# Recurrent branch of a hybrid encoder block: score blocks by 2 and by 8 in one step, a group's outputs and transposes in one step each

## The chip, the core and the metric

The kernel runs on one core of a Trainium2 chip. The metric is the device time of one execution in microseconds (us); the time of a kernel is the median of its runs. The engines of the core are TensorE (PE in the profile, with PEld for the loading of weights into it), VectorE (DVE), ScalarE (ACT), GpSimd (POOL) and SyncE (SP), which issues most of the loads.

## What is computed

One block over 256 tokens of width 2048: an HGRN2 recurrence and a chunked attention side by side, gated and merged, then a squared-ReLU MLP. All inputs are float32. The change lies in the recurrence, whose eight heads have keys and values of width 128:

```python
f = jax.nn.sigmoid(hf)
g = lb + (1.0 - lb) * f
log_g = jnp.log(g)
kk = 1.0 - g
q = jax.nn.silu(hq) * (HG_DK ** -0.5)
...
b = jnp.cumsum(gc, axis=2)
o_inter = jnp.einsum('bhtk,bhkv->bhtv', qc * jnp.exp(b), S)
diff = b[:, :, :, None, :] - b[:, :, None, :, :]
decay = jnp.exp(jnp.where(causal[:, :, None], diff, -jnp.inf))
scores = jnp.einsum('bhtk,bhtsk,bhsk->bhts', qc, decay, kc)
o_intra = jnp.einsum('bhts,bhsv->bhtv', scores, vc)
...
o = rms_norm(o, hg_norm_w) * jax.nn.silu(hg)
```

`hq`, `hf`, `hi` (the values) and `hg` (the output gate) are column blocks of the normed input times `w_in`.

## The kernel before

A float32 product is made of products of rounded parts. `weights` loads pieces of a weight from SP's queue into `raw`, ScalarE rounds each to `wh` (L91), VectorE subtracts to get `wl` (L92), and these two run ahead of TensorE through six `raw` and four `wh` and `wl` buffers at high priority. `gemm` (`hi`, `hg`) issues three matmuls for each k-tile and half of the tokens (L136 to L138), six to a k-tile; `gemm_t` (`hf`, `hq`, `aq`, `ak`) puts the channels on the partitions and issues two high products (L178) and two low ones (L183) to a k-tile.

The recurrence is worked out for pairs of heads, four of them (0 to 3); pairs 0 and 1 are group 0, pairs 2 and 3 group 1. Instead of carrying a state from chunk to chunk the kernel makes whole score matrices of 128 by 128 tokens, and one of the second half of the tokens against the first. They are put together from blocks:

- `diagonal` (L367) makes single tokens and their neighbours from `q` and `kk`.
- `factors(i, B)` (L376) makes, for blocks by B = 2, 8 and 32 tokens, the decayed keys `kl` and queries `qr` on VectorE with exponentials on ScalarE. The last instruction of `qr` is L404.
- `level(i, B)` (L407) multiplies them: for each of two heads a tile `ps` of one PSUM bank, two float32 matmuls into it (L415, each of which the profile shows as two instructions), and three predicated copies by VectorE into the score matrix `sd` (L422).
- `factors128` (L424) and `level128` (L443) do the same for the second half against the first, with matmuls at L447 and a copy to `so` by ScalarE (L449).
- `hgrn_out` (L466) has `outputs` (scores times values into `po`, L478 and L479; a square on ScalarE, L483; a sum, a small scaling and a power on VectorE, VectorE and POOL, L484, L98 and L99; four products with the factor and the gate `gw` on VectorE, L490) and `finish` (four transposes into `tpo`, L498, split into the two parts of the activation `ya`).

PSUM has eight banks: two accumulators of two banks for the weight products, two banks `ps_tp` for transposes and the last scores, two banks `ps_sm` for scores and outputs.

None of these steps runs as a stage of its own. They are put into a queue, `behind`, by `later`, each with a gap, and the products take them out: `tick` is called ahead of every k-tile with 2 by `gemm` and with 1 by `gemm_t`, and issues the first step of the queue when its gap is used up; what a tick overshoots is not carried over. So the small matmuls of a step stand in TensorE's program between two k-tiles of a weight product. `scores` (L523) queues the seven steps of a pair, `group` (L541) the outputs of a group, and hands back the transposes to be queued later.

The instructions are given to the engines in this order by a scheduler, which may put an instruction of higher priority, or one that is ready, ahead of another on the same engine. Semaphores are set by it too. `po` and `ps` are tiles of pools with two buffers, `osq` has one.

Of the kernel before, what the change touches and what calls it, by code (L numbers as in the profile page):

```python
# [8 lines left out]
F32 = mybir.dt.float32  # L9
# [7 lines left out]
P = 128  # L17
T = 256
NM = T // P
# [17 lines left out]
def bc(ap, pos, n):  # L37

    dims = [list(d) for d in ap.ap]
    dims.insert(pos, [0, n])  # L40
    return bass.AP(tensor=ap.tensor, offset=ap.offset, ap=dims)
# [9 lines left out]
def tile_hybrid_block(  # L51
# [14 lines left out]
    ps_acc, ps_tp, ps_sm = [cm.__enter__() for cm in ps_cms]  # L66
# [85 lines left out]
    def later(*steps):  # L152
        behind.extend([n, f] for n, f in steps)
# [10 lines left out]
    def gemm_t(rhs, w, n0, nkt, what):  # L164

        acc = new_acc(what)
        for a in weights(w, n0, nkt, T, what):
            tick(1)
            mm_t(acc, rhs, nkt, *a)
        return acc  # L170
# [168 lines left out]
    def v_chunk(g):  # L339
        acc = gemm(xT, w_in_n, C_HI + g * NC, KD, f"hi{g}")  # L340
        vs = []
        for m in range(NM):
            v = hp.tile([P, NC], F32, name=f"v{g}{m}", tag="tok", bufs=7)
            nc.scalar.activation(v, acc[:, m, :], AF.Copy, scale=rstd[:, m:m + 1])
            vs.append(v)
        return vs

    def hg_chunk(g):
        acc = gemm(xT, w_in_n, C_HG + g * NC, KD, f"hg{g}")
        gws = []  # L350
        for m in range(NM):
            s = hp.tile([P, NC], F32, name=f"gw{g}{m}", tag="tok", bufs=7)
            nc.scalar.activation(s, acc[:, m, :], AF.Sigmoid, scale=rstd[:, m:m + 1])
            nc.vector.scalar_tensor_tensor(s, acc[:, m, :], rstd[:, m:m + 1], s, op0=ALU.mult, op1=ALU.mult)
            s3 = s.rearrange("p (h d) -> p h d", d=DK)
            nc.vector.tensor_tensor(s3, s3, bc(hgw, 1, NH), op=ALU.mult)
            gws.append(s)
        return gws

    def hgrn_scores(n, made):  # L360

        kk, b, q = made["kk"], made["b"], made["q"]
        sd = hp.tile([P, 2, NM, P], F32, name=f"sd{n}", tag="sd", bufs=2)
        so = hp.tile([P, 2, P], F32, name=f"so{n}", tag="so", bufs=2)
# [42 lines left out]
        def level(i, B):  # L407
            kl, qr, _, _ = held[i]
            klf = kl.rearrange("p n v b -> p (n v b)")
            qrf = qr.rearrange("p n k b -> p (n k b)")  # L410
            for h in range(2):
                ps = ps_sm.tile([P, NM, 192], F32, name=f"ps{n}_{B}{h}", tag="sm")
                for m in range(NM):
                    a = 2 * h + m
                    nc.tensor.matmul(ps[:, m, :], klf[:, a * P:(a + 1) * P], qrf[:, a * 192:(a + 1) * 192],  # L415
                                     start=True, stop=True)
                dst = sd[:, h].rearrange("p m (n w) -> p m n w", w=4 * B)
                src = ps.rearrange("p m (n w) -> p m n w", w=6 * B)
                mask = masks[:, i, :].rearrange("p (n w) -> p n w", w=6 * B).bitcast(I32)
                for d0, k0, k1 in ((1, 0, 3), (2, 3, 5), (3, 5, 6)):  # L420
                    k = slice(k0 * B, k1 * B)
                    nc.vector.copy_predicated(dst[:, :, :, d0 * B:], bc(mask[:, :, k], 1, NM), src[:, :, :, k])  # L422
# [20 lines left out]
        def level128():  # L443
            kc, ql = held["128"]
            ps = ps_tp.tile([P, 2, P], F32, name=f"ps{n}_128", tag="tp")
            for h in range(2):
                nc.tensor.matmul(ps[:, h, :], kc[:, h].rearrange("p v b -> p (v b)"),  # L447
                                 ql[:, h].rearrange("p v b -> p (v b)"), start=True, stop=True)
            nc.scalar.copy(so, ps)  # L449

        f = [lambda i=i, B=B: factors(i, B) for i, B in enumerate(LEVELS)]
        l = [lambda i=i, B=B: level(i, B) for i, B in enumerate(LEVELS)]

        def first():
            diagonal()
            f[0]()

        def final():
            l[2]()
            level128()  # L460

        return (sd, so), [first, f[1], l[0], f[2], l[1], factors128, final]

    ya = []

# [38 lines left out]
    def fq(u):  # L504
        if u == 0:
            f, z = f0, z0
        elif u == 1:
            f, z = f1, z1
        else:
            f, z = h2(f"f{u}"), h2(f"zq{u}")  # L510
            add_parts(f, gemm_t(xT, w_in_t, C_HF + u * T, KD, f"hf{u}"))
            add_parts(z, gemm_t(xT, w_in_t, C_HQ + u * T, KD, f"hq{u}"))
        made = {}

        def decay():
            made["g"], made["kk"], made["b"] = hf_pair(u, f)

        def query():
            made["q"] = hq_pair(u, z, made["g"])

        return made, decay, query

    def scores(n, made, gap, first=None, between=()):  # L523

        sc = []
        steps = []

        def one(i):
            if not i:
                out, fs = hgrn_scores(n, made)  # L530
                sc.extend(out)
                steps.extend(fs)
            steps[i]()

        todo = [(gap if i or first is None else first, lambda i=i: one(i)) for i in range(7)]
        for at, f in between:
            todo.insert(at, (gap, f))
        later(*todo)
        return sc

    def group(g, s0, s1, vs, gws, gap, gap2):  # L541
        parts = {}

        def outputs(h0, sc):
            parts[h0] = hgrn_out(g, h0, sc, vs, gws)
            parts[h0][0]()

        later(*[(gap, lambda h0=h0, sc=sc: outputs(h0, sc)) for h0, sc in ((0, s0), (2, s1))])
        return [(gap2, lambda h0=h0: parts[h0][1]()) for h0 in (0, 2)]

    ya += [new_act(f"ya{g}") for g in range(2)]
    a0, a1 = fq(0), fq(1)
    a0[1]()
    a0[2]()
    s0 = scores(0, a0[0], 5, 15, ((5, a1[1]), (8, a1[2])))
    vs0 = v_chunk(0)
    s1 = scores(1, a1[0], 4)
    gws0 = hg_chunk(0)
    turns0 = group(0, s0, s1, vs0, gws0, 6, 6)
    a2 = fq(2)  # L560
    later((3, a2[1]), (3, a2[2]), *turns0)
    s2 = scores(2, a2[0], 4)
    a3 = fq(3)
    later((3, a3[1]), (3, a3[2]))
    vs1 = v_chunk(1)
    s3 = scores(3, a3[0], 4)
    gws1 = hg_chunk(1)
    later(*group(1, s2, s3, vs1, gws1, 3, 6))
    acc_q = [gemm_t(xT, w_in_t, C_AQ + i * T, KD, f"aq0{i}") for i in range(2)]
    while behind:  # L570
        tick(9)
# [639 lines left out]
```

## Time and profile before

| | |
|---|---|
| time, median of 3 runs | 1389.49 us (1389.38 to 1389.76) |
| profiled execution: time | 1389.94 us |
| profiled execution: span of the core | 1388.1 us |
| granted TensorE clock, mean | 0.999 |
| first and last score matmul (L371, L415) | 62.3 and 206.1 us |
| score blocks, L415: instructions, median duration | 96, 326 ns |
| transposes of the outputs, L498: instructions, mean duration | 16, 272 ns |
| products hi0 and hg0 | from 53 to 102 us |
| products hf2, hq2, hf3, hq3 | from 102 to 157 us |
| products hi1 and hg1, then aq | from 157 to 211 us, from 211 us |

The times in the profile are microseconds from the start of the span, durations of one instruction nanoseconds where a view says "mean". Matmuls are pipelined: the recorded durations of neighbours overlap, so what one costs is read from the distance between starts. In a timeline a row gives the start, the duration of the whole row, the engine, the line of the kernel, the operation, the tiles as out<-in, the shapes, and in brackets the idle time before it with what ended it.

### The profile page before, as it was taken

The numbers are of one execution on the slowest core, as the hardware profiler recorded it, in microseconds if no ns is written. First come the engines' busy times: TensorE is split into PE (matmuls) and PEld (weight loads), VectorE is DVE, ScalarE is ACT, GpSimd is POOL, SyncE is SP. The second block draws the span as 40 slices with busy tenths as digits, with TensorE's granted clock in tenths as the row PEclk, the third lists the DMA queues.
The fourth block names the chain that finished last, engine by engine and source line by source line (L and its number), as shares of the span: only waits on it lengthen the run. The fifth ranks groups of instructions, "written<-read, shape, count | busy, mean of one in ns | idle before, by whom it ended". The sixth has DMA issues, their size and how long they took to land.

```text
span 1388.1 us, 18593 instructions
## 1 busy us (share of the span) xinstructions
PE 1376.7 (99%) x6550; PEld 1143.5 (82%) x6550; DVE 1137.7 (82%) x1417; ACT 922.7 (66%) x1185; POOL 143.4 (10%) x227
## 2 busy tenths in 40 slices
PE   9999999999999999999999999999999999999997
PEld 8889888878778888888888888888888888888886
DVE  7897988876878775698998977879877888878886
ACT  6765645665676664346777766678666876668864
POOL 3000001101100000001211011200011001110200
PEclk9999999999999999999999999999999999999999
DMA  9654446685669886558979789988899889998892
GB/s 328 235 178 141 163 166 239 169 284 169 175 199 284 261 266 226 189 168 273 301 215 310 245 259 300 261 255 244 251 298 295 248 223 263 276 297 265 255 276 105
DMA packets 124077, 331.61 MB, mean 239 GB/s; under 512 B 11072, under 2 KB 11840, under 8 KB 123600
## 3 DMA queue, kind: packets, MB, share of 16 engines
q1 hardware_dynamic: 103696, 265.59, 54.4%
q0 software_dynamic: 19568, 64.04, 23.5%
q8 instruction: 51, 0.84, 0.2%
q10 hardware_dynamic: 720, 0.81, 0.2%
q14 instruction: 42, 0.34, 0.1%
HBM read 271.67 MB, written 10.49 MB: 203 GB/s over the span
## 4 chain that ended last, share of the span: by engine, by line
PE 89%; DMA 5%; DVE 3%; issue 2%; ACT 1%; POOL 0%; POOLq 0%; SPq 0%; ACTq 0%; DVEq 0%
PE acc_ak L178 2%; PE acc_aq L178 2%; PE acc_hf L178 2%; PE acc_hq L178 2%; PE ps L415 1%; PE acc_ak L183 1%; PE acc_hg L137 1%; PE acc_hi L137 1%; PE acc_bb L136 1%; PE acc_hi L138 1%; PE acc_hg L136 1%; PE acc_bb L137 1%; PE acc_ba L136 1%; PE acc_hi L136 1%; PE acc_ba L138 1%
## 5 line engine op out<-in xcount | busy, mean ns | idle before, releaser
L178 PE MATMUL acc_aq<-act_x,wh_aq 128*128 128x512 f32 x128 | 41.7, 402 | 0.0
L178 PE MATMUL acc_hf<-act_x,wh_hf 128*128 128x512 f32 x128 | 40.8, 400 | 0.1
L178 PE MATMUL acc_hq<-act_x,wh_hq 128*128 128x512 f32 x128 | 40.7, 400 | 0.0
L178 PE MATMUL acc_ak<-act_x,wh_ak 128*128 128x512 f32 x128 | 40.4, 397 | 0.0
L91 ACT CAST wh_bb<-raw_bb 128x1024 fp32r<-128x1024 f32 x16 | 16.9, 1054 | 23.3 <-PE acc_ba L138 17.7
L92 DVE TENSOR_TENSOR wl_bb<-raw_bb,wh_bb 128x1024 fp32r<-128x1024 f32 x16 | 19.6, 1223 | 14.8 <-ACT wh_bb L91 14.8
L91 ACT CAST wh_ba<-raw_ba 128x1024 fp32r<-128x1024 f32 x16 | 16.8, 1052 | 19.9 <-PE acc_bb L138 13.8
L92 DVE TENSOR_TENSOR wl_aq<-raw_aq,wh_aq 128x1024 fp32r<-128x1024 f32 x16 | 19.5, 1222 | 12.5 <-ACT wh_aq L91 12.5
L92 DVE TENSOR_TENSOR wl_ba<-raw_ba,wh_ba 128x1024 fp32r<-128x1024 f32 x16 | 19.5, 1223 | 11.6 <-ACT wh_ba L91 11.6
L183 PEld LDWEIGHTS acc_hq<-act_x,wl_hq 128*128 128x128 f32 x128 | 23.4, 188 | 6.6 <-DVE wl_hq L92 1.4
L91 ACT CAST wh_aq<-raw_aq 128x1024 fp32r<-128x1024 f32 x16 | 16.7, 1051 | 17.1 <-PE acc_hg L138 7.3
L183 PEld LDWEIGHTS acc_hf<-act_x,wl_hf 128*128 128x128 f32 x128 | 23.4, 188 | 5.5 <-DVE wl_hf L92 0.3
L183 PEld LDWEIGHTS acc_ak<-act_x,wl_ak 128*128 128x128 f32 x128 | 23.5, 188 | 5.3
L183 PEld LDWEIGHTS acc_aq<-act_x,wl_aq 128*128 128x128 f32 x128 | 23.3, 188 | 5.1 <-issue 0.3
L92 DVE TENSOR_TENSOR act_u<-tp_u,act_u 128x512 fp32r<-128x512 f32 x32 | 21.9, 685 | 4.7 <-ACT act_u L91 4.2
L183 PE MATMUL acc_hq<-act_x,wl_hq 128*128 128x256 f32 x128 | 24.7, 280 | 1.0 <-DVE wl_hq L92 1.0
L136 PE MATMUL acc_hg<-wh_hg,act_x 128*128 128x512 f32 x64 | 25.6, 400 | 0.0
L183 PE MATMUL acc_aq<-act_x,wl_aq 128*128 128x256 f32 x128 | 25.6, 284 | 0.0
L136 PE MATMUL acc_hi<-wh_hi,act_x 128*128 128x512 f32 x64 | 25.5, 399 | 0.0
L92 DVE TENSOR_TENSOR wl_hf<-raw_hf,wh_hf 128x1024 fp32r<-128x1024 f32 (+2 forms) x21 | 20.5, 976 | 6.1 <-ACT wh_hf L91 5.7
L91 ACT CAST wh_ak<-raw_ak 128x1024 fp32r<-128x1024 f32 x16 | 16.8, 1051 | 12.9 <-PE acc_aq L178 5.5
L136 PE MATMUL acc_bb<-wh_bb,act_yb 128*128 128x512 f32 x64 | 25.2, 393 | 0.0
(1928 smaller groups left out, 5237.3 us busy)
## 6 DMA issues: line engine op xcount, KB each, us to landing
raw_hi<-in_w_in_n_dram SPq DMA_DIRECT2D x16, 512.0 KB, 4.5
raw_hg<-in_w_in_n_dram SPq DMA_DIRECT2D x16, 512.0 KB, 3.5
raw_aq<-in_w_in_t_dram SPq DMA_DIRECT2D x16, 512.0 KB, 3.7
raw_ak<-in_w_in_t_dram SPq DMA_DIRECT2D x16, 512.0 KB, 4.8
raw_ba<-in_w_branch_a_dram SPq DMA_DIRECT2D x16, 512.0 KB, 4.6
raw_bb<-in_w_branch_b_dram SPq DMA_DIRECT2D x16, 512.0 KB, 4.7
raw_hf<-in_w_in_t_dram SPq DMA_DIRECT2D x12, 512.0 KB, 3.6
raw_hq<-in_w_in_t_dram SPq DMA_DIRECT2D x12, 512.0 KB, 4.0
```

The lines of the kernel that those rows point to most:

```text
L91: casts[:] = [(copy or nc.scalar.copy)(hi, src)]
L92: return nc.vector.tensor_tensor(lo, src, hi.bitcast(F32), op=ALU.subtract)
L136: nc.tensor.matmul(acc, hi, wh, start=first, stop=False, skip_group_check=True)
L137: nc.tensor.matmul(acc, hi, wl, start=False, stop=False, skip_group_check=True)
L138: nc.tensor.matmul(acc, lo, wh, start=False, stop=last, skip_group_check=True)
L178: nc.tensor.matmul(acc[:, cb, :], wh[:, cb * P:(cb + 1) * P], r.rearrange("p u t -> p (u t)"), start=kt == 0, stop=last)
L183: nc.tensor.matmul(acc[:, cb, 0:T], wl[:, cb * P:(cb + 1) * P], r[:, 0, :], start=False, stop=False)
L415: nc.tensor.matmul(ps[:, m, :], klf[:, a * P:(a + 1) * P], qrf[:, a * 192:(a + 1) * 192], start=True, stop=True)
```

## The change

The steps of a pair become six: the multiplications of the blocks by 2 and by 8 are issued in one step, `near`, after both their factors; those by 32 and `level128` stay one step, now called `far`. The two `ps` tiles of the blocks by 8 come from `ps_tp` instead of `ps_sm`. The outputs of a group's two pairs are one step, `both`, and their transposes one step, `finish`. The gaps are changed with it: from 5 and 4 to 6 for scores, from 6 to 8 for the transposes; the gaps of the outputs, 6 and 3, stay, but there is one of them to a group instead of two. The places at which pair 1's decay and query are put into the queue of pair 0 move from 5 and 8 to 4 and 7.

```diff
@@ level
-                ps = ps_sm.tile([P, NM, 192], F32, name=f"ps{n}_{B}{h}", tag="sm")
+                home, tag = (ps_tp, "tp") if i == 1 else (ps_sm, "sm")
+                ps = home.tile([P, NM, 192], F32, name=f"ps{n}_{B}{h}", tag=tag)
@@ hgrn_scores
-        def final():
+        def near():
+            l[0]()
+            l[1]()
+
+        def far():
             l[2]()
             level128()
-        return (sd, so), [first, f[1], l[0], f[2], l[1], factors128, final]
+        return (sd, so), [first, f[1], near, f[2], factors128, far]
@@ scores
-        todo = [(gap if i or first is None else first, lambda i=i: one(i)) for i in range(7)]
+        todo = [(gap if i or first is None else first, lambda i=i: one(i)) for i in range(6)]
@@ group
-        later(*[(gap, lambda h0=h0, sc=sc: outputs(h0, sc)) for h0, sc in ((0, s0), (2, s1))])
-        return [(gap2, lambda h0=h0: parts[h0][1]()) for h0 in (0, 2)]
+        def both():
+            outputs(0, s0)
+            outputs(2, s1)
+
+        def finish():
+            for h0 in (0, 2):
+                parts[h0][1]()
+
+        later((gap, both))
+        return [(gap2, finish)]
@@ tile_hybrid_block
-    s0 = scores(0, a0[0], 5, 15, ((5, a1[1]), (8, a1[2])))
+    s0 = scores(0, a0[0], 6, 15, ((4, a1[1]), (7, a1[2])))
-    s1 = scores(1, a1[0], 4)
+    s1 = scores(1, a1[0], 6)
-    turns0 = group(0, s0, s1, vs0, gws0, 6, 6)
+    turns0 = group(0, s0, s1, vs0, gws0, 6, 8)
-    s2 = scores(2, a2[0], 4)
+    s2 = scores(2, a2[0], 6)
-    s3 = scores(3, a3[0], 4)
+    s3 = scores(3, a3[0], 6)
-    later(*group(1, s2, s3, vs1, gws1, 3, 6))
+    later(*group(1, s2, s3, vs1, gws1, 3, 8))
```

## The prediction

> **What bounds the kernel now.** I read the page's engine shares and its chain first, then who TensorE (PE) waited for, then the stretch of the recurrent branch in windows, then its instructions one by one.
>
> ```profile
> PE 1376.7 (99%) x6550; PEld 1143.5 (82%) x6550; DVE 1137.7 (82%) x1417; ACT 922.7 (66%) x1185; POOL 143.4 (10%) x227
> ```
>
> ```profile
> PE 89%; DMA 5%; DVE 3%; issue 2%; ACT 1%; POOL 0%; POOLq 0%; SPq 0%; ACTq 0%; DVEq 0%
> ```
>
> ```profile
> PE ps_warm L81 <- DVE warm L79: 1.1, 1, 1.1
> PE acc_hq L183 <- DVE wl_hq L92: 1.0, 1, 1.0
> PE tpp L618 <- DVE sb L614: 0.3, 2, 0.2
> PE acc_ga0c L136 <- ACT acc_ga0c L759: 0.3, 1, 0.3
> ```
>
> The columns of the last are the sum, the times and the longest wait in us. TensorE is the bound, and none of its waits lies in the recurrent branch (62 to 226 us). What the change can win there is only TensorE time that is neither a matmul at full rate nor a wait: the seams between the stream of weight products and the small float32 matmuls put in between. What it can lose is a wait that does not exist today. VectorE (DVE) is the candidate for that:
>
> ```profile
> 157.00:183.00 26.00, 26.00 (x125) 22.24 (x124) 25.96 (x66) 17.68 (x24) 0.00 (x0) 1.00 0.45 147
> ```
>
> Behind the stretch and its length stand PE, weight loads, VectorE, ScalarE, POOL, the granted clock and DMA: VectorE is busy 25.96 of 26.00 us, the clock is 1.00. TensorE does not notice, since VectorE runs ahead of it.
>
> **The seam of a score step.** This is the first pair's blocks by 2 (L415, eight instructions: two for each float32 matmul), start and duration:
>
> ```profile
> 71.55 0.39 PE L138 MATMUL acc_hi<-wh_hi,act_x 128*128 128x512 f32 x1
> 71.78 1.46 PE L415 MATMUL ps<-qr,kl 128*128 128x192 f32 x8
> 72.94 0.53 PE L136 MATMUL acc_hi<-wh_hi,act_x 128*128 128x512 f32 x1
> 73.31 0.40 PE L137 MATMUL acc_hi<-wl_hi,act_x 128*128 128x512 f32 x1
> 73.54 0.39 PE L138 MATMUL acc_hi<-wh_hi,act_x 128*128 128x512 f32 x1
> ```
>
> Starts count, since durations overlap. Undisturbed, a product matmul starts 0.23 us after the last (71.55 to 71.78, 73.31 to 73.54). The eight take 72.94 - 71.78 = 1.16 us, 0.145 each; the first product matmul behind them takes 73.31 - 72.94 = 0.37 instead of 0.23. The seam is 0.14 us, at the return only. Two blocks in one step keep all sixteen small instructions and pay it once: 0.14 x 4 pairs = **0.56 us** saved.
>
> **The seams of outputs and transposes.**
>
> ```profile
> 130.64 0.61 PE L479 MATMUL po<-v,sd 128*128 128x128 f32 x4
> ...
> 131.90 0.70 PE L178 MATMUL acc_hf<-act_x,wh_hf 128*128 128x512 f32 x2
> 132.44 0.40 PE L183 MATMUL acc_hf<-act_x,wl_hf 128*128 128x256 f32 x2
> 132.68 0.62 PE L178 MATMUL acc_hf<-act_x,wh_hf 128*128 128x512 f32 x2
> 133.14 0.40 PE L183 MATMUL acc_hf<-act_x,wl_hf 128*128 128x256 f32 x2
> ...
> 145.88 0.60 PE L498 MATMUL tpo<-ident,o 128*128 128x128 f32 x4
> 146.24 0.71 PE L178 MATMUL acc_hq<-act_x,wh_hq 128*128 128x512 f32 x2
> 146.79 0.40 PE L183 MATMUL acc_hq<-act_x,wl_hq 128*128 128x256 f32 x2
> ```
>
> Two high products take 133.14 - 132.68 = 0.46; behind an output step 132.44 - 131.90 = 0.54, behind a pair's transposes 146.79 - 146.24 = 0.55. Each seam is 0.08, and each of the two groups loses one of either kind: 0.08 x 4 = **0.32 us**. The step itself is 131.90 - 130.64 = 1.26, the transposes 146.24 - 145.88 = 0.36; both are unchanged. All seams together: **0.88 us**, the whole gain there is to have. No matmul, eviction, exponential or DMA is removed.
>
> **What moves, and what it could wait for.** The gaps count ticks: one for a k-tile of a transposed product (133.14 - 132.44 = 0.70 us), two for a k-tile of the others. Counted through the queue of steps with its rounding, the places become:
>
> Blocks by 2 of the first pair stay ahead of k-tile 13 of hi0, and the blocks by 8, six k-tiles later before, now stand right behind them. Their factors are VectorE work:
>
> ```profile
> 70.40 1.22 DVE L92 TENSOR_TENSOR wl_hg<-raw_hg,wh_hg 128x1024 fp32r<-128x1024 f32 x1 [0.23 <-ACT wh_hg L91]
> 71.54 0.55 DVE L402 TENSOR_TENSOR qr<-q,er 128x384 f32<-128x384 f32 x1
> 72.01 0.68 DVE L382 TENSOR_TENSOR el<-b 128x512 f32<-128x512 f32 x1
> 72.61 0.42 DVE L403 TENSOR_TENSOR qr<-qr,rr 128x256 f32<-128x256 f32 x1
> 72.94 1.22 DVE L92 TENSOR_TENSOR wl_hg<-raw_hg,wh_hg 128x1024 fp32r<-128x1024 f32 x1
> 74.08 0.28 DVE L404 TENSOR_TENSOR qr<-qr,rr 128x128 f32<-128x128 f32 x1
> ```
>
> The last piece of the blocks by 8 (L404) is done at 74.36, and TensorE would want it at 72.94: a wait of **1.42 us**, behind which the rest of hi0 queues. Against the full price: L382 of the next factors (blocks by 32) stands between L402 and L403 of this one, so the order on an engine is arranged by what is ready, not by the code alone; if TensorE's order is arranged so too, product matmuls go ahead of the blocks by 8, and only the 0.14 of this one seam is lost. Bounds 0.14 to 1.42; I take 0.2, as that row shows the arranging. In the other three pairs a whole gap of six ticks (4.2 us) lies between the factors and the joint step, and VectorE works on them long before; second and fourth pair I put at nothing, the third, inside the full stretch quoted above, between 0 and 0.7 (one k-tile), and take 0. The twelve predicated copies behind a joint step queue on VectorE ahead of weight splits (wl); what covers these is their lead, as the first wl_hg above ends at 71.62 and TensorE starts on it at
>
> ```profile
> 77.17 0.39 PE L136 MATMUL acc_hg<-wh_hg,act_x 128*128 128x512 f32 x1
> ```
>
> which is 5.5 us later. Without that cover a split (1.22) would come on the path. Accumulators: the blocks by 8 take the transposes' buffers, so four are in use at once and none is waited for; two outputs fill the two score buffers, whose next user comes over 10 ticks later; so nothing.
>
> The outputs of the first group are transposed 14 ticks after them (9.8 us, the second pair 0.4 later), and the chain behind outputs is long: before, the second pair was left by TensorE at the first row and ready at the end of the second,
>
> ```profile
> 137.42 0.70 PE L178 MATMUL acc_hf<-act_x,wh_hf 128*128 128x512 f32 x2
> ```
>
> ```profile
> 147.70 0.34 DVE L490 SCALAR_TENSOR_TENSOR o<-po,ro,gw 128x128 f32<-128x128 f32 x1
> ```
>
> 148.04 - 137.42 = 10.6 us against 10.2: 0 to 0.4 of wait. The second group has less room. Before:
>
> ```profile
> 216.83 0.70 PE L178 MATMUL acc_aq<-act_x,wh_aq 128*128 128x512 f32 x2
> ...
> 225.73 0.60 PE L498 MATMUL tpo<-ident,o 128*128 128x128 f32 x4
> ```
>
> ```profile
> 217.11 0.60 ACT L483 ACTIVATE osq<-po 128x512 f32<-128x512 f32 x1 [0.65 <-PE po L479]
> ```
>
> ```profile
> 221.77 0.16 DVE L98 TENSOR_SCALAR os<-os 128x4 f32<-128x4 f32 x1
> 223.06 0.87 DVE L490 SCALAR_TENSOR_TENSOR o<-po,ro,gw 128x128 f32<-128x128 f32 x3 [1.12 <-POOL ro L99]
> ...
> 225.57 0.34 DVE L490 SCALAR_TENSOR_TENSOR o<-po,ro,gw 128x128 f32<-128x128 f32 x1
> ```
>
> Chain 225.91 - 216.83 = 9.1 us, room 225.73 - 216.83 = 8.9: just in time. Now the room is 8 ticks and the first pair's transposes, 8 x 0.70 + 0.36 = 6.0. At the old length TensorE waits **3.1 us**, with the rest of the aq products behind it. It need not be so long: ScalarE had its square at 217.11, yet the next small step came at 221.77. The second pair's chain lay behind the first pair's on VectorE and behind the gate of hg1, which TensorE finishes two and five k-tiles ahead of the two outputs before, but six and the last scores ahead of them after. From 221.77 on the chain needs 4.1. Bounds 0 to 3.1; I take 0.3, since the shorter end is what the work needs. The outputs of the fourth pair also follow its last scores more closely, 3 ticks and the third pair's outputs behind, 2.1 + 1.26 = 3.4 us. Six copies have to be through by then:
>
> ```profile
> 206.00 1.58 DVE L422 COPY_PREDICATED sd<-masks,ps 128x192 f32<-128x192 int32 x6
> ```
>
> With a split ahead of them, 1.58 + 1.22 = 2.8: nothing. POOL's power instructions move with the outputs, and its bias loads for the attention are issued behind the last of them, now earlier; SP's queue is not passed.
>
> **Sum.** -0.88 + 0.2 + 0.3 = -0.4 us. The profiled execution has a span of 1388.1 and a time of 1389.94, 1.84 outside the span; the median of the runs is 0.45 below it. Applied to the median: 1389.49 - 0.4 = **1389.1**.
>
> **Rivals.**
> 1. *One wait at full price.* Only the first pair's: -0.88 + 1.42 = +0.5, 1390.0. Only the second group's: -0.88 + 3.1 = +2.2, 1391.7. For it: VectorE's order above, and a chain that was just in time. Against: the arranging, and the gate's work that leaves the chain.
> 2. *Slower: the transposes of the second group wait for their outputs, the chain being as long as in the first group.* 10.6 - 6.0 = 4.6 of wait, -0.88 + 4.6 = +3.7, 1393.2. It decides over 0.2% (2.8 us) from a chain of 6.0 + 0.9 + 2.8 = 9.7 us. For it: one square buffer and two outputs at once, so that ScalarE and VectorE hold each other up in order. Against: the second group has no factors of a next pair beside it.
>    The Trainium skill (TensorE: Matmul & The Clock Gate, Part 1: The HAM clock gate) says that TensorE's clock falls to half after an idle window of about 3.4 us. By that rule such a wait would cost another 1.7 us (an estimate: one window at half rate), 1395; no run here shows it yet.
> 3. *The steps are taken apart again* by the arranging, or the seam stays between two blocks: no gain, no wait, 1389.5. For it: L382 above. Against: every step of TensorE that I followed stands at its counted k-tile.
> 4. *Faster by over 0.2%.* Beyond 0.88 there would have to go 1.9 us of waits, and after the start-up TensorE's are 0.3 + 0.3. Only a changed order in the later stages could do it, 1386.5.
>
> **How the numbers follow.** About 0.2%, 2.8 us, is what a measurement of this kernel can tell from no change. Forecast 0.46 (its own range 1388.4 to 1390.0); rival 1: 0.19; rival 2: 0.20; rival 3: 0.10; rival 4: 0.05. Rivals 1 and 3 lie within the bound, so the same: 0.46 + 0.19 + 0.10 = 0.75; slower 0.20, faster 0.05. The range, 1387.8 to 1393.0, leaves out rival 4 and most of rival 2, and holds the bounds of both waits taken singly.
>
> **What would show it.** Right: in each pair sixteen L415 instructions in a row, about 2.33 us, and one matmul of 0.37 behind them; 24 output instructions and then eight transposes in a row; no new line among TensorE's waits; the hpool stage ending 0.4 to 0.9 us earlier. Wrong: a gap ahead of the blocks by 8 near 73 us, or ahead of L498 in the aq products with L490 as its releaser, or a wl split that comes late in the stretch where VectorE is full.

## The result, and the profile after

The changed kernel takes **1390.76 us** (median of 22 runs, 1390.44 to 1394.22), the kernel before 1389.32 on the same chip (22 runs, 1388.4 to 1390.94): a ratio of 1.0012, with a 95% interval of 1.0007 to 1.0018. That is +1.44 us (by the interval 1.0 to 2.5), inside the bound of 0.2% and inside the range, but the sign is not the forecast one: a loss that can be told from nothing, where a gain of 0.4 was expected.

The page of the changed kernel, busy time by engine and the chain that ended last:

```profile
PE 1376.5 (99%) x6550; PEld 1143.3 (82%) x6550; DVE 1138.3 (82%) x1417; ACT 922.6 (66%) x1184; POOL 143.2 (10%) x227
...
PE 93%; DMA 2%; DVE 2%; ACT 1%; issue 1%; POOL 0%; POOLq 0%; SPq 0%; ACTq 0%; DVEq 0%
```

The engine totals show nothing: the same counts as before, but for one record of ScalarE (1184 against 1185). The difference stands in the list of whom TensorE waited for (sum in us, times, longest), of the changed kernel:

```profile
PE acc_hq L183 <- DVE wl_hq L92: 1.1, 1, 1.1
...
PE ps L416 <- DVE qr L404: 1.0, 1, 1.0
...
PE tpo L503 <- DVE o L495: 0.2, 1, 0.2
```

The first line was there before. L416 (L415 before) and L503 (L498) are new, and they are the only two in the recurrent branch, where nothing was waited for before. The list of this profile has three more that the first profile of the kernel before has not: `acc_hf` (0.6 and 0.4), which lie in the start-up ahead of hi0 and which further profiles of the kernel before show too, and `acc_avc` (0.3), far behind the branch.

To price them I use one stretch of the trace, from the first matmul of hi0 to the first of ak, and call it M. Columns of a timeline: start, duration, engine, line, operation, tiles, shapes, count. The kernel before, then the changed one:

```profile
52.77 0.39 PE L136 MATMUL acc_hi<-wh_hi,act_x 128*128 128x512 f32 x1
...
236.63 0.62 PE L178 MATMUL acc_ak<-act_x,wh_ak 128*128 128x512 f32 x2
```

```profile
53.49 0.39 PE L136 MATMUL acc_hi<-wh_hi,act_x 128*128 128x512 f32 x1
...
239.59 0.62 PE L178 MATMUL acc_ak<-act_x,wh_ak 128*128 128x512 f32 x2
```

M is 236.63 - 52.77 = 183.86 before and 239.59 - 53.49 = 186.10 after: **+2.24 us**. M repeats to 0.03 us from profile to profile of a kernel, while times scatter by 1 us and more, so M carries the argument and the time checks it. The waits that make M grow, and why no gain stands against them, can be seen in the rows.

**First pair's scores.** TensorE of the changed kernel (in brackets: idle time before the row, and what ended it):

```profile
72.49 1.46 PE L416 MATMUL ps<-qr,kl 128*128 128x192 f32 x8
73.65 0.53 PE L136 MATMUL acc_hi<-wh_hi,act_x 128*128 128x512 f32 x1
75.16 1.57 PE L416 MATMUL ps<-qr,kl 128*128 128x192 f32 x8 [0.97 <-DVE qr L404]
76.43 0.53 PE L137 MATMUL acc_hi<-wl_hi,act_x 128*128 128x512 f32 x1
76.79 0.39 PE L138 MATMUL acc_hi<-wh_hi,act_x 128*128 128x512 f32 x1
```

and VectorE at the same time:

```profile
72.27 0.55 DVE L402 TENSOR_TENSOR qr<-q,er 128x384 f32<-128x384 f32 x1
72.74 0.69 DVE L382 TENSOR_TENSOR el<-b 128x512 f32<-128x512 f32 x1
73.34 0.42 DVE L403 TENSOR_TENSOR qr<-qr,rr 128x256 f32<-128x256 f32 x1
73.68 1.22 DVE L92 TENSOR_TENSOR wl_hg<-raw_hg,wh_hg 128x1024 fp32r<-128x1024 f32 x1
74.81 0.29 DVE L404 TENSOR_TENSOR qr<-qr,rr 128x128 f32<-128x128 f32 x1
```

VectorE's order is that of the kernel before, with the high-priority split of L92 between L403 and L404. The blocks by 8 want L404's result at 73.65 + 0.37 = 74.02, the price of one returning matmul; it is done at 75.10, and they start at 75.16, 1.14 late. The arranging did put a product matmul between the halves of the joint step, but only one.

**Outputs and transposes.** First group's transposes (L503):

```profile
146.45 0.93 PE L503 MATMUL tpo<-ident,o 128*128 128x128 f32 x7
147.62 0.33 PE L503 MATMUL tpo<-ident,o 128*128 128x128 f32 x1 [0.24 <-DVE o L495]
147.70 0.71 PE L178 MATMUL acc_hq<-act_x,wh_hq 128*128 128x512 f32 x2
```

with what VectorE did just before the last one,

```profile
146.08 1.22 DVE L92 TENSOR_TENSOR wl_hq<-raw_hq,wh_hq 128x1024 fp32r<-128x1024 f32 x1
147.22 0.35 DVE L495 SCALAR_TENSOR_TENSOR o<-po,ro,gw 128x128 f32<-128x128 f32 x1
```

again a split ahead of the one small instruction that TensorE needs. Second group, in the aq products (TensorE leaves the third pair's outputs at 218.56, in a row not shown):

```profile
220.04 0.39 PE L178 MATMUL acc_aq<-act_x,wh_aq 128*128 128x512 f32 x1
220.45 0.68 PE L484 MATMUL po<-v,sd 128*128 128x128 f32 x4
...
221.78 0.48 PE L178 MATMUL acc_aq<-act_x,wh_aq 128*128 128x512 f32 x1
...
225.82 1.36 PE L503 MATMUL tpo<-ident,o 128*128 128x128 f32 x8
226.94 0.70 PE L178 MATMUL acc_aq<-act_x,wh_aq 128*128 128x512 f32 x2
```

Eight transposes take 0.79 us where they wait for nothing (the run `room` below). Here they take 147.70 - 146.45 = 1.25 and 226.94 - 225.82 = 1.12: 0.46 and 0.33 too long. The fourth pair's outputs start 0.41 behind the product matmul ahead of them instead of 0.23: 0.18. Together 0.97.

The step `both` of the second group was taken apart: nine product matmuls stand between the third pair's outputs and the fourth's. VectorE's last copy into the fourth pair's score matrix ends just ahead of them, at 220.30:

```profile
220.08 0.22 DVE L423 COPY_PREDICATED sd<-masks,ps 128x64 f32<-128x64 int32 x1
```

The six copies that the prediction put at 2.8 us took from 214.32 to 220.30, 6.0 us, with the gate's products, a split and the sum of the third pair's squares between them. So in the changed kernel six of the eight returns went, not all: those of three score steps, of the first group's outputs and of both groups' transposes.

**Seams.** The joint step of the second pair, which waits for nothing, in the changed kernel:

```profile
112.93 2.77 PE L416 MATMUL ps<-qr,kl 128*128 128x192 f32 x16
115.39 0.76 PE L178 MATMUL acc_hf<-act_x,wh_hf 128*128 128x512 f32 x2
115.99 0.40 PE L183 MATMUL acc_hf<-act_x,wl_hf 128*128 128x256 f32 x2
```

and the end of the same row in a narrower window:

```profile
115.20 0.49 PE L416 MATMUL ps<-qr,kl 128*128 128x192 f32 x2
```

The sixteen and the return cost 2.46 + (0.60 - 0.46) = 2.60 us, which is 0.1625 an instruction and just twice the 1.16 + 0.14 = 1.30 of eight before. The prediction's own sign for being right, 2.33 us for the sixteen, came out at 2.46. The narrow row tells why it saw a seam: the last two instructions have 115.39 - 115.20 = 0.19 us to the next start, not 0.33. The first product matmul's recorded start lies early, in the last small instruction's time, and the missing 0.14 comes back behind it. Counted so, it belongs to the small instructions.

### The profile page after: what moved, and what is told of

The parts are those of the page before. It is cut to its first block, busy times and chain, and to the rows that moved or that the text cites. A ratio compares the mean times of both kernels' runs of the same rounds, so it can differ in the third digit from the quotient of the medians.

```text
span 1390.0 us, 18587 instructions
## 1 busy us (share of the span) xinstructions
PE 1376.5 (99%) x6550; PEld 1143.3 (82%) x6550; DVE 1138.3 (82%) x1417; ACT 922.6 (66%) x1184; POOL 143.2 (10%) x227
## 4 chain that ended last, share of the span: by engine, by line
PE 93%; DMA 2%; DVE 2%; ACT 1%; issue 1%; POOL 0%; POOLq 0%; SPq 0%; ACTq 0%; DVEq 0%
PE acc_ak L178 2%; PE acc_aq L178 2%; PE acc_hq L178 2%; DMA raw_hf<-in_w_in_t_dram 2%; PE acc_hf L178 1%; PE acc_ak L183 1%; PE tp_u L109 1%; PE ps L416 1%; PE acc_bb L137 1%; PE acc_hg L136 1%; PE acc_ba L137 1%; PE acc_ba L138 1%; PE acc_bb L138 1%; PE acc_hg L137 1%; PE acc_hg L138 1%; PE acc_bb L136 1%
## 5 line engine op out<-in xcount | busy, mean ns | idle before, releaser
L92 DVE TENSOR_TENSOR wl_bb<-raw_bb,wh_bb 128x1024 fp32r<-128x1024 f32 x16 | 19.6, 1224 | 14.8 <-ACT wh_bb L91 14.8
L92 DVE TENSOR_TENSOR wl_ba<-raw_ba,wh_ba 128x1024 fp32r<-128x1024 f32 x16 | 19.6, 1224 | 12.3 <-ACT wh_ba L91 12.3
L92 DVE TENSOR_TENSOR wl_aq<-raw_aq,wh_aq 128x1024 fp32r<-128x1024 f32 x16 | 19.5, 1223 | 10.7 <-ACT wh_aq L91 10.7
L92 DVE TENSOR_TENSOR wl_hf<-raw_hf,wh_hf 128x1024 fp32r<-128x1024 f32 (+2 forms) x21 | 20.3, 969 | 7.8 <-ACT wh_hf L91 7.6
L92 DVE TENSOR_TENSOR act_u<-tp_u,act_u 128x512 fp32r<-128x512 f32 x32 | 21.9, 686 | 4.7 <-ACT act_u L91 4.2
L91 ACT CAST wh_hg<-raw_hg 128x1024 fp32r<-128x1024 f32 x16 | 16.7, 1046 | 13.2 <-PE acc_hg L138 6.2
```

What stands on the lines that cost most here:

```text
L91: casts[:] = [(copy or nc.scalar.copy)(hi, src)]
L92: return nc.vector.tensor_tensor(lo, src, hi.bitcast(F32), op=ALU.subtract)
```

## The experiments

In most expectations A is the theory that joining saves nothing and only its waits cost, and B the prediction's, that a return costs 0.14 or 0.08; C, X and Y are explained where they stand. All kernels compute what the kernel before computes. The table has each run's time with its ratio to the kernel before on the same chip, and the profiled span cut in three: up to hi0, M, and from ak's first matmul to the end.

| run | us, median (runs) | ratio, 95% | to hi0 | M | behind |
|---|---|---|---|---|---|
| before | 1389.32 (22) | | 52.77 | 183.86 | 1151.5 |
| after | 1390.76 (22) | 1.0012, 1.0007 to 1.0018 | 53.49 | 186.10 | 1150.4 |
| seam_halves | 1390.85 (11) | 1.0014, 1.0005 to 1.0023 | 53.17 | 185.28 | 1150.8 |
| twice_all | 1394.06 (5) | 1.0037, 1.0025 to 1.0050 | 52.78 | 189.06 | 1150.5 |
| pair0_apart | 1389.74 (11) | 1.0004, 0.9995 to 1.0013 | 52.71 | 184.85 | 1150.2 |
| split_behind | 1390.41 (11) | 1.0008, 0.9999 to 1.0017 | 53.63 | 185.50 | 1150.2 |
| near_early | 1390.87 (11) | 1.0014, 1.0005 to 1.0023 | 52.87 | 186.08 | 1150.2 |
| outs_apart | 1390.99 (11) | 1.0013, 1.0004 to 1.0022 | 52.92 | 186.15 | 1150.1 |
| room_outs | 1390.01 (11) | 1.0007, 0.9998 to 1.0016 | 52.51 | 185.06 | 1150.3 |
| room | 1388.64 (11) | 0.9996, 0.9987 to 1.0004 | 52.97 | 183.79 | 1150.0 |
| room_again | 1388.58 (11) | 0.9992, 0.9983 to 1.0001 | 52.94 | 183.77 | 1150.3 |
| before_again | 1390.11 (11) | 1.0007, 0.9998 to 1.0016 | 52.52 | 183.85 | 1150.1 |
| before_c | 1389.29 (1) | | 53.09 | 183.83 | 1150.5 |
| before_d | 1389.44 (1) | | 52.99 | 183.86 | 1150.8 |
| before_e | 1390.01 (1) | | 52.97 | 183.85 | 1151.5 |
| after_again | 1391.70 (1) | | 53.13 | 186.09 | 1150.7 |

### Is there a seam? More returns (seam_halves), more small matmuls (twice_all)

seam_halves is the kernel before with the two heads of each score block two ticks apart: twelve returns more, no instruction more (gaps adapted so that the places stay).

```diff
-        l = [lambda i=i, B=B: level(i, B) for i, B in enumerate(LEVELS)]
+        l = [[lambda i=i, B=B, h=h: level(i, B, (h,)) for h in range(2)] for i, B in enumerate(LEVELS)]
...
-        return (sd, so), [first, f[1], l[0], f[2], l[1], factors128, final]
+        return (sd, so), [first, f[1], *l[0], f[2], *l[1], factors128, l[2][0], final]
```

> The kernel before, with the two heads of every score block (L415) put a k-tile (two ticks) apart instead of next to each other: the same instructions, 12 more returns from small matmuls to the product stream. M is the distance from the first matmul of hi0 to the first of ak0 in the trace, 183.86 us in the kernel before and 186.10 in the changed one. Theory A (there is no seam: a 128x192 instruction costs 0.163 us wherever it stands, its neighbours' modelled starts only hid that): M 183.9 +- 0.2, time as before within 0.3 us. Theory B (a seam of 0.14 us at each return, as the prediction had it): M 185.5, time 0.8 to 1.7 us longer.

M came out at 185.28, +1.42: near B's number, far from A's. The rows give another cause. Transposes of the second group in this run:

```profile
225.23 0.49 PE L498 MATMUL tpo<-ident,o 128*128 128x128 f32 x3
225.47 0.36 PE L183 MATMUL acc_aq<-act_x,wl_aq 128*128 128x256 f32 x1
226.54 0.33 PE L498 MATMUL tpo<-ident,o 128*128 128x128 f32 x1 [0.70 <-DVE o L490]
```

From 225.47 to 226.54 are 1.07 us for half a low pair, which takes 0.12: 0.95 is a wait that the moved steps made. What is left, 1.42 - 0.95 = 0.47 for twelve returns, is 0.04 each on average, not 0.14; it is a difference, so whatever else the moved steps cost is in it. It isn't spread evenly: from the start of hf2 to that of hi1, with three of the twelve, the run takes 55.12 us and the kernel before 55.15. A's "nothing" is missed by that much, B's size by more; the run by its time alone would have misled.

twice_all issues the eight instructions of L371 (128x192, one step for each of four pairs) twice: 32 more.

```diff
-                for m in range(NM):
+                for m in [*range(NM)] * (2 if True else 1):
```

> The kernel before with every matmul of the single-token blocks (L371) issued twice, 32 small instructions more. Theory A (0.163 us for each, wherever it stands): M 183.86 + 5.2 = 189.1. Theory B (0.145 and a seam that stays the same): M 188.5. For the time: if a late branch is given back between 410 and 500 us as the first pair of traces looked, 0.8 us less than M grows, +4.4; if that was the jitter of loads, +5.2.

M grew by 5.20 us, 5.20 / 32 = 0.1625 an instruction, although no return was added. That is the same figure as 2.60 / 16 and 1.30 / 8, so eight instructions account for the whole 1.30, and nothing of it is left for the return: the 0.14 is part of them. The Trainium skill (Perfetto Trace Analysis, Engine Utilization) gives TensorE's output rate as 307.2 G elements a second, halved for FP32_LOW_HIGH: an estimate of 128 x 192 / 153.6 G = 0.160 us. If that is the mode of these instructions, which no view here names, it agrees with the 0.1625; it has no term for a return.

### The first pair: apart, earlier, or without the split

pair0_apart is the changed kernel with the first pair's blocks by 8 issued behind the factors for 32, three k-tiles later.

```diff
+        def blocks32():
+            f[2]()
+            l[1]()
+
+        if n == 0:
+            return (sd, so), [first, f[1], l[0], blocks32, factors128, far]
```

> The changed kernel, with the blocks by 8 of the first pair alone moved behind the factors of the blocks by 32, three k-tiles later; every other step stays at its place. Theory A (no seam; the branch loses 1.25 us to the wait for L404 of the first pair, 0.43 to the transposes of group 0 and 0.59 in the aq products): M 186.10 - 1.25 = 184.85, no wait of L416 for L404, time about 0.5 us above before (some 0.8 us of what is lost is given back between 410 and 500 us). Theory B (seams of 0.14, and waits of 2.24 + 0.88 = 3.1 us): M 184.99 at that wait; it differs from A too little here. Theory C (the loss comes from the changed gaps in general, not from that wait): M stays at 186.1.

M is 184.85, 1.25 less than in the changed kernel, and of TensorE's new waits only L503's (0.2 in the list) is left. 1.25 is the whole price of the wait for L404: the 1.14 above, and some 0.1 that the blocks by 8 themselves take longer behind a pause (75.16 to 76.43 is 1.27, against 1.16).

near_early asks whether an earlier joint step costs more: the first pair's comes one k-tile sooner.

```diff
-        todo = [(gap if i or first is None else first, lambda i=i: one(i)) for i in range(6)]
+        gaps = [first or gap] + [gap] * 5
+        if n == 0:
+            gaps[2:4] = 4, 8
+        todo = [(d, lambda i=i: one(i)) for i, d in enumerate(gaps)]
```

> The changed kernel with the first pair's joint score step one k-tile of hi0 earlier (gap 4 instead of 6, the next gap 8 instead of 6, so that what follows keeps its place). Theory A (TensorE waits there for the last factor of the blocks by 8, whose end VectorE sets and not TensorE): the wait grows by the k-tile that is taken away, 6 x 0.227 = 1.36 us, at L404 again, M 187.3 to 187.5. Theory C (the loss is no wait at this place): M 186.1.

A miss: M is 186.08, unchanged. TensorE in this run:

```profile
70.50 1.46 PE L416 MATMUL ps<-qr,kl 128*128 128x192 f32 x8
...
73.18 0.39 PE L136 MATMUL acc_hi<-wh_hi,act_x 128*128 128x512 f32 x1
74.53 1.57 PE L416 MATMUL ps<-qr,kl 128*128 128x192 f32 x8 [0.96 <-DVE qr L404]
```

The blocks by 2 did come sooner, but seven product matmuls now stand between the halves, and the blocks by 8 start 74.53 - 52.87 = 21.66 us behind hi0, as in the changed kernel (75.16 - 53.49 = 21.67). As these rows read, the arranging holds them back to where it takes L404 to be done, and the wait is what the chip's L404 is later than that place; one run doesn't show it as a rule.

split_behind leaves the changed order and holds back one split of hg's weights until L404 is issued (lines behind it move by 3).

```diff
-                with tc.high_priority(offset=2000):
+                with ExitStack() as es:
+                    es.enter_context(tc.high_priority(offset=2000))
+                    if what == "hg0" and k0 == 2:
+                        es.enter_context(tc.issue_after(hold[0, 1].ins))
...
-            nc.vector.tensor_tensor(qr[:, :, 5, :], qr[:, :, 4, :], bc(rr[:, :, 1], 2, B), op=ALU.mult)
+            hold[n, i] = nc.vector.tensor_tensor(qr[:, :, 5, :], qr[:, :, 4, :], bc(rr[:, :, 1], 2, B), op=ALU.mult)
```

> The changed kernel, with one piece of VectorE work moved: the split of the weights wl_hg that stood between L403 and L404 of the first pair (1.22 us at 73.68 in the changed kernel's profile) is issued behind that L404. Everything is computed as before. Theory A (TensorE's wait of 0.97 at the first pair's blocks by 8 comes from this split on VectorE, since the joint step leaves only one product matmul between the two halves): L404 ends about 0.8 us earlier (the split's 1.13 of start-to-start time gives way to 0.34 for the next addition), the wait shrinks to 0.3 to 0.5, and from the first matmul of the recurrent branch's first product to the first of ak it takes 185.4 us, plus or minus 0.2 (186.1 in the changed kernel, 183.9 in the one before); the waits of the transposes (0.43 and 0.59 of excess) stay. Time about 1390.0. Rival (the wait is set by the chain L402, L403, L404 itself, or by TensorE's own order): the wait stays at about 1.0 and the stretch at 186.1; time 1390.7.

M is 185.50, 0.60 less. TensorE and VectorE in this run (L419, L406, L407 are L416, L403, L404):

```profile
72.62 1.46 PE L419 MATMUL ps<-qr,kl 128*128 128x192 f32 x8
74.48 1.57 PE L419 MATMUL ps<-qr,kl 128*128 128x192 f32 x8 [0.40 <-DVE qr L407]
```

```profile
73.47 0.42 DVE L406 TENSOR_TENSOR qr<-qr,rr 128x256 f32<-128x256 f32 x1
73.81 0.42 DVE L396 TENSOR_TENSOR er<-b 128x256 f32<-128x256 f32 x1
74.14 0.28 DVE L407 TENSOR_TENSOR qr<-qr,rr 128x128 f32<-128x128 f32 x1
74.34 1.22 DVE L92 TENSOR_TENSOR wl_hg<-raw_hg,wh_hg 128x1024 fp32r<-128x1024 f32 x1
```

L407 comes 0.67 behind L406 instead of 1.47, TensorE's listed wait falls from 0.97 to 0.40, and about half of the 1.25 is gone. So the split on VectorE is half of this wait. An addition for the next factors (L396) took its place and holds L407 up by 74.14 - 73.81 = 0.33 again; that the rest is the factors themselves, late for a joint step at this place, is the likely reading and was not tried. The sixteen now stand in a row, too.

### Outputs and transposes: apart, or with room

outs_apart takes the outputs and transposes of the changed kernel apart again, as two steps each (gaps 3, 4 and 6).

```diff
...
-        later((gap, both))
-        return [(gap2, finish)]
+        later((gap, lambda: outputs(0, s0)), (3, lambda: outputs(2, s1)))
+        return [(gap2, lambda: parts[0][1]()), (6, lambda: parts[2][1]())]
```

> The changed kernel, with outputs and transposes of the two pairs of a group as two steps again, 16 ticks between a pair's outputs and its transposes in group 0; the score steps stay at their places. Theory A: M 186.10 - 0.43 - 0.59 = 185.1, and the wait of 1.0 us for L404 stays; time 0.2 to 0.6 us above before. Theory B: four returns more, +0.32, M 185.4. Theory C (outputs cost nothing): M 186.1.

A miss: 186.15, not 185.1. The aq products got their time back, but the first group's transposes, placed for this run, waited more than in the changed kernel (0.93 against 0.24):

```profile
149.80 0.49 PE L503 MATMUL tpo<-ident,o 128*128 128x128 f32 x3
151.22 0.33 PE L503 MATMUL tpo<-ident,o 128*128 128x128 f32 x1 [0.93 <-DVE o L495]
```

It tells nothing of joining, only that the place decides. room_outs keeps everything joined and gives room instead: transposes three and five ticks later, the second group's outputs three.

```diff
-    turns0 = group(0, s0, s1, vs0, gws0, 6, 8)
+    turns0 = group(0, s0, s1, vs0, gws0, 6, 11)
...
-    s2 = scores(2, a2[0], 6)
+    s2 = scores(2, a2[0], 6, 3)
...
-    later(*group(1, s2, s3, vs1, gws1, 3, 8))
+    later(*group(1, s2, s3, vs1, gws1, 6, 13))
```

> The changed kernel with more room for outputs and transposes only (3 and 5 ticks more ahead of the transposes, 3 more ahead of the outputs of group 1); the joint score step of the first pair stays where it waits for L404. Theory A: M 186.10 - 0.43 - 0.59 = 185.1 +- 0.15, the wait of 1.0 us for L404 stays and the one of L503 goes. Theory C (the waits at the transposes come from what the first wait shifted, so they go only with it): M 186.1.

M is 185.06: 1.04 less, where the rows above summed to 0.97. The wait of L503 is gone, that of L416 stays at 1.0.

room has this and the first pair's joint step two k-tiles later; room_again is the same kernel a second time.

```diff
...
+        if n == 0:
+            gaps[2:4] = 10, 2
...
```

> The changed kernel with everything joined as it is, and only more room: the first pair's joint score step two k-tiles later, the transposes 3 ticks later in group 0 and 5 in group 1, the outputs of group 1 three ticks later. Theory A (no seam, so nothing to gain from joining): no wait left, M as in the kernel before, 183.9 +- 0.2, time as before within 0.3 us. Theory B: M 183.86 - 0.88 = 183.0.

> The changed kernel with room for every joint step (the first pair's scores two k-tiles later, the transposes three and five ticks later, the second group's outputs three ticks later), as in the run named room, taken a second time, since its time stood within the noise of the kernel before. Theory A (joining saves nothing, only its waits cost): the stretch from the branch's first product to ak is 183.8 us, plus or minus 0.1, as in the kernel before (183.86), and the time lies within 0.6 us of the kernel before's. Rival B (each of the twelve removed returns is worth about 0.07 us, the prediction's 0.88 in all): 183.0, and a time 0.9 us below the kernel before's.

TensorE in room, first pair and second group:

```profile
74.69 2.76 PE L416 MATMUL ps<-qr,kl 128*128 128x192 f32 x16
77.15 0.53 PE L136 MATMUL acc_hi<-wh_hi,act_x 128*128 128x512 f32 x1
...
228.91 1.03 PE L503 MATMUL tpo<-ident,o 128*128 128x128 f32 x8
229.70 0.70 PE L178 MATMUL acc_aq<-act_x,wh_aq 128*128 128x512 f32 x2
```

Everything is joined, nothing waits in the branch, and M is 183.79 and 183.77: 0.07 to 0.09 below the kernel before. This is what joining is worth, against the 0.88 of B. (Rival B of room_again speaks of twelve removed returns; there are eight: four score steps, two of outputs and two of transposes.) The effects add up: 1.25 + 1.04 = 2.29, and from 186.10 to 183.79 are 2.31. The time of room_again, 0.95 below the kernel before, is outside A's 0.6 and at B's number, but its interval still holds no difference at all, and M says that it doesn't come from the branch.

### Where the time and M differ

M grew by 2.24, the median by 1.44, and room's two medians lie 0.47 and 0.95 below the kernel before's on their chips (1389.11 and 1389.53), with an M that is equal to 0.1. before_again was a first look at the scatter.

> The kernel before, unchanged, for a second trace. M 183.86 +- 0.1. If TensorE waits again about 0.5 us each for ScalarE's copies in the products ga2 and gb0 (around 434 and 475 us), what the changed kernel gave back there belongs to it; if these waits are gone, they are jitter of the loads.

Its median is 1390.11, 1.0007 of the same kernel's: the times alone do not resolve 0.8 us. But behind ak its profile is 1.3 us shorter than the first. Three more profiles, and one of the changed kernel, asked whether that is a habit of the kernel before.

> The kernel before, unchanged, for a further profile. The stretch from the branch's first product to ak grew by 2.24 us with the change, the time by 1.44 only, so some 0.8 is given back elsewhere. Behind ak the first profile of the kernel before has 1151.5 us to the end of the span, with two waits of weight loads (acc_ga2c for u_ga 0.6, acc_gb0c for u_gb 0.5); its second profile 1150.1 without them; eight profiles of the changed kernel and its variants 1150.0 to 1150.4, without them. Theory X (the kernel before usually has these waits, the changed order usually not: the give-back): two at least of three further profiles of the kernel before show 1150.9 to 1151.8 and the waits. Rival Y (chance of the loads, no tie to the change): none or one of three. The stretch up to ak is 183.85 in each by both.

> As for the run before_c: the kernel before once more. Theory X: 1150.9 to 1151.8 us behind the first matmul of ak, with the two waits for u_ga and u_gb. Rival Y: 1150.0 to 1150.4, without them. The stretch up to ak 183.85 by both.

> As for the runs before_c and before_d. Theory X: 1150.9 to 1151.8 us behind the first matmul of ak, with the waits for u_ga and u_gb. Rival Y: 1150.0 to 1150.4, without them. The stretch up to ak 183.85 by both.

> The changed kernel, unchanged, for a further profile. Both theories: the stretch up to ak 186.1 us, behind it 1150.0 to 1150.5, no wait for u_ga or u_gb. If these waits come here, theory X falls, whatever the three of before show. The start-up, up to the branch's first product, was 53.49 us in the first profile of the changed kernel against 52.5 to 52.8 in the two of before: if it belongs to the changed order and not to the loads, it is 53.3 to 53.6 again; if not, 52.5 to 53.0.

Weight loads of TensorE that waited, in before_e and in after_again:

```profile
PEld acc_ga2c L136 <- ACT u_ga L759: 0.5, 1, 0.5
```

```profile
PEld acc_gb0c L136 <- ACT u_gb L772: 0.3, 1, 0.3
```

One of the three lies above 1150.9 (1151.5), and after_again has such a wait as well: by the terms set ahead, X falls. Over all profiles something may be left of it. The wait of `acc_ga2c` for `u_ga` stands in four of the five profiles of the kernel before (0.3 to 0.6) and in seam_halves, which has its order (0.7), and in none of the nine of the changed kernel and its variants; what came in after_again is the other one, for `u_gb`. Behind ak the five have 1150.9 on average (1150.1 to 1151.5), the nine 1150.3 (1150.0 to 1150.7). But the wait does not set that time alone: before_c has it at 0.6 and 1150.5. The start-up, 53.49 in the first profile of the changed kernel, was 53.13 in the second, and so is not tied to the change. What gives back the rest of the 0.8 us, or whether it is scatter of the medians (+2.24 lies in the interval of 1.0 to 2.5), stays open.

## Why the prediction was wrong, by its steps

- **The bound** was right: TensorE, with no wait in the branch, so that a wait newly made there goes through in full: from hi0's start to the end, room_outs takes 1.12 us less than the changed kernel (186.10 + 1150.41 = 1336.51 against 185.06 + 1150.33 = 1335.39), for 1.04 less in M, though the part behind ak scatters by as much between profiles. The plainer sign is twice_all: its median is 5.02 us longer than that of the kernel before on its chip (1394.06 against 1389.04), for 5.20 more in M.
- **The seams, -0.56 and -0.32: the step that failed.** It took the late second product behind the eight for a cost of switching that is paid once to a return. The recorded start of the first matmul behind a run of these instructions lies 0.14 early; n instructions have to be counted up to the second matmul behind them. So counted they cost 0.1625 each in a row of 8 or 16, and joining keeps all of them. Worth 0.07 to 0.09 in M, not 0.88. The forecast's whole gain hung on it, with no row that held twice as many score instructions at one return.
- **First pair's blocks by 8, 0.2 taken of 0.14 to 1.42: the wait named rightly, its size not.** It cost 1.25, near the upper bound, and in size this term was missed by more (1.05) than the seams (0.8). That product matmuls are put between was right; that they would hide the wait was not: there was room for one, and about half of the wait goes when one split is held back. The sign set for being wrong, a gap ahead of the blocks by 8, is what came.
- **The other three pairs at nothing:** right, the list of waits has no L416 but the first pair's.
- **First group's transposes, 0 to 0.4, with 0 in the sum:** 0.46, just over the upper end. The chain from the outputs (TensorE leaves them at 136.61, in a row not shown) to the last L495 (147.57) took 11.0 where 10.6 was reckoned; its last link stood behind a split, but no run moved that split, so what it is worth is not shown.
- **Second group, 0.3 of 0 to 3.1:** 0.33 at the transposes and 0.18 at the outputs ahead of them. The chain did get shorter, as argued: from the last outputs (221.78) to the end of the transposes (226.94) are 5.2 us, against 9.1 before. That the 0.3 fits so well is luck in part: the room was 225.82 - 221.78 = 4.0 and not 6.0, because the fourth pair's outputs came late. That these wait for nothing was wrong by 0.18; by the rows they wait for the copies, which were through after 6.0 us and not 2.8, but no run tried it alone.
- **Buffers and weight splits at nothing:** right; behind hi0's start, no accumulator or wl of the branch is among the waits.
- **Sum.** -0.88 + 0.2 + 0.3 = -0.4 foretold; -0.1 + 1.25 + 1.04 = 2.2 in M, +1.44 in the time. Without the seams the same two terms for the waits would have given +0.5, and the right sign. That 1390.76 lies inside the range confirms nothing: the range was wide enough for either wait at its full price.

Of the rivals, the first (one wait at full price, 1390.0) is the nearest, and with it came a ninth of the second's wait (0.33 + 0.18 of 4.6). The first pair's joint score step and the second group's outputs were taken apart (rival 3), by one product matmul and by nine, but unlike rival 3 not without a wait. The long wait that the rule of the Trainium skill needs (TensorE: Matmul & The Clock Gate, Part 1: The HAM clock gate) did not come, so no run shows that rule at work here: the longest idle time of TensorE in the branch is 0.97 us, and the granted clock was 0.998 or 0.999 in the profiled execution of every run.

## What to carry to other kernels

Before a gap between two kinds of matmul is called a cost of switching, count the starts of n instructions up to the second one behind them, and compare rows with different n: a cost that grows with n belongs to the instructions. Joining two small steps of a filled engine's stream saved next to nothing here, and it made the later one's inputs due earlier; what that cost hung on one short instruction on another engine, and about half of it on the long, high-priority one that stood ahead of it. Where single times scatter by more than the effect, a stretch of the trace between two fixed matmuls, repeating here to 0.03 us, resolves it; and even then the rows decide what a difference in it is, as seam_halves shows.

## What the hardware did that was not expected

- A float32 score matmul's instruction (128x192) took 0.1625 us in rows of 8 and of 16 and when doubled (5.20 us for 32). A return to the product stream cost little beside it: 0.47 us for twelve more, 0.07 to 0.09 saved by eight fewer.
- Behind a pause the same eight instructions took 1.27 us to the next start instead of 1.16, so a wait of 1.14 cost 1.25.
- Between profiles of the kernel before, the start-up ahead of hi0 differed by up to 0.6 us (52.52 to 53.09), the part behind ak by 1.4 (1150.1 to 1151.5), and the branch between them by 0.03.
